# A diffusion backbone on one Trainium2 core: first-layer modulation sums taken from TensorE to ScalarE and GpSimd

## Chip, cores and metric

The kernel runs on one core of a Trainium2 chip. The metric is the device time of one execution in microseconds, lower is better; three executions were timed and their median is used. One more execution was profiled.

## The reference

Two layers of a transformer-like backbone work on 256 latent tokens (`xl`) and 256 context tokens (`xc`) of width 1024. Ahead of each layer a vector of six modulation parts is made for either kind of token, a product of one vector with a 1024 x 6144 matrix:

```python
mod_l = (jax.nn.silu(c) @ ada_w[l] + ada_b[l])[:, None, :]
mod_c = (jax.nn.silu(c_ctx) @ ada_w[l] + ada_b[l])[None, None, :]
sh1_l, sc1_l, g1_l, sh2_l, sc2_l, g2_l = jnp.split(mod_l, 6, axis=-1)
...
hl = modulate(rmsnorm(xl, norm_attn_g[l]), sh1_l, sc1_l)
...
xl = xl + g1_l * yl
xl = xl + g2_l * ffn(modulate(rmsnorm(xl, norm_ffn_g[l]), sh2_l, sc2_l))
```

The change concerns parts 2 to 4 of layer 0: the gate `g1` of the mixer's output, and shift and scale of the second norm. They are wanted only when layer 0's mixer is done; parts 0 and 1 are wanted at once, part 5 and all of layer 1 later.

## The kernel before

Everything is float32. A product is made of three TensorE passes over split operands (`mm3`, L296): weights come as 128 x 1024 tiles (`raw`), ScalarE copies the high part (`whi`, L269) and VectorE subtracts the rest (`wlo`, L270). Layer 0 (`layer0`, L528) projects the 512 normed tokens on 29 column blocks (`proj(m)`, L602): first q and k, then v (L612 to L626, weights `evv`), dt, the scan's input `xBC` (twelve blocks, each followed by a convolution on VectorE, L747 to L753), and z. Between the `xBC` blocks lie the steps of the attention over eight heads (`nattn`, L638): scores on TensorE, bias and maximum on VectorE, exponentials on ScalarE, transposes on TensorE. Behind that come the scan's states (`ssm1`, L817), its output (`ssm2`, L856, where GpSimd makes the tiles `xd` at L895), the output projection and the feed-forward.

The modulation runs in pieces, in the background. `tick()` (L442) takes the next step of the generator `bg`. `ada(0, 1)` (L345) loads sixteen 128 x 1024 tiles of `ada_w` (`araw`, two buffers) and multiplies each on TensorE with the two vectors as stationary operand (`ada_mm`, L313, four matmuls in a tick, each on its own 32 columns of the array); `ada4` (L379) does the same with eight tiles for part 4. `TKP` says after which projections a tick is made, `TKS` that one follows each step of `ssm2`; `need` (L445) draws the rest when a part is wanted. A second generator `bg1` (`ada_sums`, L401) is already written the other way: VectorE multiplies a tile by a column of the vector and adds it to an accumulator (L422, L424), and at the end of a group TensorE only sums over the partitions (L430), followed by four transposes (L371). It serves part 5 of layer 0 and layer 1, and is drawn in the feed-forward.

A scheduler lays down the order of each engine's instructions. All loads go out through one queue (SP), in order; a load that waits for its buffer holds those behind it. The small scratch tiles `hp` have four buffers.

```python
def tick():
    next(bg, None)
...
TKP, TKO, TKS = range(6, 29, 3), 0, 1
```

Of the kernel before, what the change touches and what calls it, by code (L numbers as in the profile page):

```python
# [10 lines left out]
F32 = mybir.dt.float32  # L11
# [7 lines left out]
P = 128  # L19
D = 1024  # L20
KD = 8
# [66 lines left out]
def prepare(x, c, ctx, c_ctx, ada_w, ada_b, norm_attn_g, norm_ffn_g,  # L88
            ev_w_in, ev_w_out, na_rpb, ssm_conv_w, ssm_conv_b, ssm_dt_bias, ssm_a_log, ssm_d, ssm_norm_g,
            ffn_w1, ffn_w3, ffn_w2,  # L90
            od_w_in, od_w_out, swa_sink, ret_log_decay, ret_gn_g, ret_gn_b,
            moe_router, moe_w1, moe_w3, moe_w2, final_g):
    cat = np.concatenate
    A = {}
    A.update(_CT)
    xt = cat([ctx[0], x[0]], axis=0).T
    A["xt"] = xt.reshape(KD, P, 512).transpose(1, 0, 2)
    cc = np.zeros((P, KD, 32), np.float32)
    cc[:, :, 0] = _cols(c_ctx)
    cc[:, :, 1] = _cols(c[0])  # L100
    cc[:, 0, 16] = 1.0
    A["cc"] = cc
    aw = ada_w.reshape(2, KD, P, 3, 2, 2, 512)
    A["ada"] = aw[0].transpose(2, 0, 4, 1, 3, 5).reshape(3, KD, 2, P, 1024)[:2]
    A["ad4"] = aw[0, :, :, 2, 0].reshape(KD, P, 1024)
    ac = aw.reshape(2, 4, 2, P, 3, 2, 2, 512).transpose(0, 4, 6, 5, 1, 3, 2, 7).reshape(2, 3, 4, 4, P, 1024)
    A["adc"] = cat([ac[0, 2, 1::2], ac[1].reshape(12, 4, P, 1024)])
    vec = [_cols(ada_b[0]), _cols(ada_b[1]),
           _cols(norm_attn_g[0]), _cols(norm_attn_g[1]), _cols(norm_ffn_g[0]), _cols(norm_ffn_g[1]),
           _cols(final_g), _cols(ssm_norm_g[0]),  # L110
           _cols(ret_gn_g[0]), _cols(ret_gn_b[0]), _cols(ssm_conv_b[0]),
           ssm_conv_w[0, :, 0, :].reshape(5, 12, P).transpose(2, 1, 0).reshape(P, 60),
           _cols(cat([ssm_dt_bias[0].reshape(-1), np.zeros(96, np.float32)]))]
    ld = ret_log_decay[0]
    vec += [np.repeat(ld.reshape(2, 4, 2).transpose(2, 0, 1), 64, axis=0).reshape(P, 8)]
    A["vec"] = cat(vec, axis=1)
    rows = [ssm_a_log[0].reshape(-1), ssm_d[0], swa_sink[0], ld.reshape(-1)]
    A["row"] = cat(rows)[None, :]
    w = ev_w_in[0]
    q, k, v, z, xbc, dt = np.split(w, np.cumsum([512, 512, 512, 1024, 1536])[:].tolist(), axis=1)  # L120
    dtp = cat([dt, np.zeros((D, 96), np.float32)], axis=1)
    bx = _blocks(cat([q, k, dtp, xbc, z], axis=1))
    bx[:48] = bx[:48].reshape(3, 2, 2, 4, P, P).transpose(2, 0, 1, 3, 4, 5).reshape(48, P, P)
    A["evx"] = _tiles(bx)
    A["evv"] = v.reshape(4, 2, P, 512).transpose(0, 2, 1, 3).reshape(4, P, 1024)
    for i in range(3):
        A["evo%d" % i] = _tiles(_blocks(ev_w_out[0, 512 * i:512 * i + 512]))
    f = cat([ffn_w1[0].reshape(D, NF, 1, P), ffn_w3[0].reshape(D, NF, 1, P)], axis=2).reshape(D, 2 * NF * P)
    A["f13"] = _tiles(_blocks(f))
    A["f2"] = _tiles(_blocks(ffn_w2[0]))  # L130
    w = od_w_in[0]
    q, k, v, rq, rk, rv, rg = np.split(w, np.cumsum([512, 128, 128, 512, 512, 1024])[:].tolist(), axis=1)
    q = q.reshape(D, 2, 4, 64).transpose(0, 2, 1, 3).reshape(D, 512)
    A["odx"] = _tiles(_blocks(cat([k, rk[:, :2 * P], q, v, rk[:, 2 * P:], rq, rg], axis=1)))
    ov = rv.reshape(2, 4, P, 4, 256).transpose(3, 0, 2, 1, 4).reshape(8, P, 1024)
    A["odv"] = ov
    wo = od_w_out[0]
    wq = wo[:512].reshape(2, 4, 64, D).transpose(1, 0, 2, 3).reshape(512, D)
    A["ods"] = _tiles(_blocks(wq))
    A["odr"] = _tiles(_blocks(wo[512:]))  # L140
    q0 = np.arange(256)
    kc = np.arange(64)
    qr, qc = q0 // 64, q0 % 64
    c0 = np.clip(qc - 8, 0, 48)
    ok = (kc[None, :] >= c0[:, None]) & (kc[None, :] < c0[:, None] + 16)
    ci = np.clip(kc[None, :] - qc[:, None] + 15, 0, 30)
    dr = np.arange(4)[None, :] - qr[:, None] + 7
    b = na_rpb[0][:, dr[:, :, None], ci[:, None, :]]
    b = np.where(ok[None, :, None, :], b, np.float32(NEG))
    A["nab"] = b.reshape(8, 2, P, 256).transpose(0, 2, 1, 3).reshape(8, P, 512)  # L150
    A["rt"] = moe_router[0].reshape(KD, P, NE).transpose(1, 0, 2)
    m13 = cat([moe_w1[0].reshape(NE, 1, 2, 4, P, 7, 512), moe_w3[0].reshape(NE, 1, 2, 4, P, 7, 512)], axis=1)
    A["m13"] = m13.transpose(0, 5, 1, 2, 4, 3, 6).reshape(NE, 7, 4, P, 2048)
    m2 = moe_w2[0].reshape(NE, 7, 2, 2, P, 1024)
    A["m2"] = m2.transpose(0, 1, 2, 4, 3, 5).reshape(NE, 7, 2, P, 2048)
    return {k: np.ascontiguousarray(v, dtype=np.float32) for k, v in A.items()}
# [11 lines left out]
def tile_backbone(ctx: ExitStack, tc: tile.TileContext, A, out, upto=99, dbg=None):  # L168
# [2 lines left out]
    NPG, NHP, NW, NA = 22, 4, 3, 2  # L171
    GN0 = 5
    WPRE = (3, 7)
    TKP, TKO, TKS = range(6, 29, 3), 0, 1
    ST = (1, 1, 1, 1, 1, 1, 1, 1, 0, 0)
    ONACT = ((0, 0), (0, 1), (1, 1))
    AHEAD, LEAD, NWT, PRE, SPL = 1, 4, 11, (1, 3, 5, 7), (1, 3)
# [164 lines left out]
            V.scalar_tensor_tensor(gs[:, l, w, s, k0:k1], mod[:, l, s, c0 + k0:c0 + k1], 1.0, vc(gname)[:, k0:k1],  # L342
                                   op0=ALU.add, op1=ALU.mult)

    def ada(l, g):  # L345
        pa = bank("ada")
        for k in range(KD):
            for half in range(2):
                ada_mm(pa, ada_load(l, g, k, half), k, 2 * half)
            yield  # L350
        ada_evac(pa, l, g, (0, 1))
        if g == 0:
            mk_gs(l, 0, "ga%d" % l)
        if g == 2:
            mk_gs(l, 1, "gf%d" % l)

    bgdone = set()

    def background():
        for it, g in ((ada(0, 1), 1), (ada4(), 2)):  # L360
            for _ in it:
                yield
            bgdone.add((0, g))

    def ada_evac2(pa, l, parts):
        n = 32 * len(parts)
# [9 lines left out]
            for s in range(2):  # L376
                V.tensor_tensor(mod[:, l, s, m:m + 4], v[:, s, j], vec[:, o + m:o + m + 4], op=ALU.add)

    def ada4():  # L379
        pa = bank("ada")  # L380
        for k in range(KD):
            raw = araw_tile()
            nc.sync.dma_start(raw, A["ad4"][k])
            ada_mm(pa, raw, k, 2 * (k % 2), 1, 6)
            if k % 2:
                yield
        sb = pool[0].tile([P, 512], F32, tag="nab", name="adas", bufs=2)
        V.tensor_copy(sb, pa)
        pt = bank("ada")
        for b in range(4):  # L390
            for i in range(2):
                T.matmul(pt[:, b * 64:(b + 1) * 64], sb[:, b * P:(b + 1) * P], ident[:, 64 * i:64 * i + 64],
                         start=i == 0, stop=i == 1)
        v = pt[:, 0:256].rearrange("p (b j t) -> p t j b", b=4, t=32)
        o = VOFF["adab0"][0] + 32
        for s in range(2):
            V.tensor_tensor(mod[:, 0, s, 32:40].rearrange("p (j b) -> p j b", j=2), v[:, s],
                            vec[:, o:o + 8].rearrange("p (j b) -> p j b", j=2), op=ALU.add)
        mk_gs(0, 1, "gf0")

    def ada_sums():  # L401
        flat = scc.rearrange("p a b -> p (a b)")
        groups = [(0, (0, 1), [(5, 0), (5, 1)])]
        groups += [(1, (0, 1), [(0, h), (1, h)]) for h in range(2)]
        groups += [(1, (1,), [(g + i, h) for h in range(2) for i in range(2)]) for g in (2, 4)]
        src = iter(range(14))
        for l, who, parts in groups:
            acc = {}
            for j in range(len(parts)):
                n = next(src)  # L410
                for s in who:
                    acc[j, s] = (pm_([P, 512]) if len(acc) < 2 else
                                 pool[0].tile([P, 512], F32, tag="nab", name="acc", bufs=2))
                for kp in range(4):
                    raw = araw_tile()
                    nc.sync.dma_start(raw, A["adc"][n, kp])
                    for k2 in range(2):
                        x = raw[:, k2 * 512:k2 * 512 + 512]
                        for s in who:
                            cs = scc[:, 2 * kp + k2, s:s + 1]  # L420
                            if (kp, k2) == (0, 0):
                                V.tensor_scalar(acc[j, s], x, cs, None, op0=ALU.mult)  # L422
                            else:
                                V.scalar_tensor_tensor(acc[j, s], x, cs, acc[j, s], op0=ALU.mult, op1=ALU.add)  # L424
# [7 lines left out]
            ada_evac2(pa, l, parts)  # L432
            if l and parts[0][0] == 0:
                mk_gs(1, 0, "ga1", 4 * parts[0][1], 4 * parts[0][1] + 4)
            if l and parts[0][0] == 4:
                mk_gs(1, 1, "gf1")
            yield

    bg = background()
    bg1 = ada_sums()  # L440

    def tick():  # L442
        next(bg, None)
# [84 lines left out]
    def layer0():  # L528
# [73 lines left out]
        def proj(m):  # L602
            pp = bank()
            proj_mm(ws, m, 8, hH, hL, pp, 0, 512)
            if m in TKP:
                tick()
            return pp

# [1372 lines left out]
```

## Time and profile before

| | |
|---|---|
| median of three executions | 2102.27 us (2098.06 to 2103.82) |
| the profiled execution | 2096.44 us, span 2094.7 us |
| TensorE (PE) busy over the span | 97% |
| VectorE (DVE), ScalarE (ACT), GpSimd (POOL) | 61%, 43%, 5% |
| mean granted TensorE clock | 0.993 of full speed |

The profiled execution is 5.8 us below the median of the three. A busy share is an average over stages with different limits; the stage that the change touches is the first 350 us.

### The profile page before, as it was taken

The page shows a single profiled execution, that of the slowest core. Times are in us where ns is not written, and L with a number is a line of the kernel's source. Part 1 is how long each engine was busy: PE and PEld are TensorE (multiplying, and loading weights), DVE is VectorE, ACT ScalarE, POOL GpSimd, SP SyncE. Part 2 cuts the span into 40 slices and gives each one's busy share as a digit, 9 for nine tenths or more (in the row PEclk, how much of TensorE's full clock was granted, in tenths as well). Part 3 has the DMA queues.
Part 4 walks back from the last instruction along what each step waited for, and adds up shares of the span by engine and source line. Part 5 has one row for each costly group of instructions (what it writes and reads, how often), then busy time and mean ns, then how long its engine had stood idle before and what let it go on. Part 6 is the DMA issues. An engine that isn't in the chain of part 4 may idle for free. (4 is left out here: it accounts for less than half of the span.)

```text
span 2094.7 us, 26701 instructions
## 1 busy us (share of the span) xinstructions
PE 2026.0 (97%) x10170; PEld 1438.0 (69%) x10170; DVE 1288.0 (61%) x1878; ACT 906.0 (43%) x1296; POOL 109.1 (5%) x148
## 2 busy tenths in 40 slices
PE   7999999889999999999999999999999999999997
PEld 4776756688777878888888888878654554545453
DVE  5366557777566664765477888887644344434443
ACT  4346525643222223544356776767532232232322
POOL 0000015600000000100101000000000000000000
PEclk9999999999999999999999999999999999999998
DMA  8422432025444674322254999999989999999994
GB/s 317 150 94 96 151 121 95 24 68 161 142 150 151 209 236 128 125 61 81 84 228 146 337 364 323 322 334 335 371 352 397 401 406 398 390 418 383 384 361 181
DMA packets 89445, 496.25 MB, mean 237 GB/s; under 512 B 10080, under 2 KB 10848, under 8 KB 46048
## 3 DMA queue, kind: packets, MB, share of 16 engines
q1 hardware_dynamic: 89312, 494.49, 64.3%
q8 instruction: 82, 1.34, 0.3%
q14 instruction: 51, 0.42, 0.1%
HBM read 493.40 MB, written 1.05 MB: 236 GB/s over the span
## 5 line engine op out<-in xcount | busy, mean ns | idle before, releaser
L270 DVE TENSOR_TENSOR w<-w 128x2048 fp32r<-128x2048 f32 (+1 forms) x186 | 384.5, 2081 | 58.7 <-ACT w L269 40.9
L269 ACT ACTIVATE w<-w 128x2048 fp32r<-128x2048 f32 (+1 forms) x186 | 320.5, 1748 | 62.2 <-DVE w L270 35.4
L269 ACT ACTIVATE whi<-raw 128x1024 fp32r<-128x1024 f32 x151 | 160.0, 1060 | 404.1 <-PE bk_mm L298 263.3
L270 DVE TENSOR_TENSOR wlo<-raw,whi 128x1024 fp32r<-128x1024 f32 x151 | 186.6, 1236 | 140.8 <-ACT whi L269 138.3
L297 PE MATMUL bk_mm<-fH,whi 128*128 128x512 f32 (+1 forms) x360 | 140.0, 390 | 2.0 <-DVE xT L518 1.2
L299 PE MATMUL bk_mm<-fH,wlo 128*128 128x512 f32 (+1 forms) x360 | 138.8, 387 | 2.1 <-DVE wlo L270 2.1
L297 PE MATMUL bk_mm<-hH,whi 128*128 128x512 f32 (+1 forms) x384 | 137.5, 361 | 2.2 <-ACT hH L269 2.2
L298 PE MATMUL bk_mm<-fL,whi 128*128 128x512 f32 (+1 forms) x360 | 139.2, 388 | 0.0
L298 PE MATMUL bk_mm<-hL,whi 128*128 128x512 f32 (+1 forms) x384 | 136.2, 355 | 0.0
L299 PE MATMUL bk_mm<-hH,wlo 128*128 128x512 f32 (+1 forms) x384 | 135.5, 354 | 0.0
L1551 PE MATMUL bk_pt<-w,xf 128*64 128x512 f32 x448 | 113.0, 601 | 0.0
L1704 ACT COPY g<-bk_ax 64x512 f32<-64x512 f32 x35 | 20.4, 582 | 207.9 <-PE bk_ax L1551 207.7
L1551 PE MATMUL bk_ax<-w,xf 128*64 128x512 f32 x448 | 107.2, 597 | 0.0
L1763 PE MATMUL bk_mm<-w,gf 128*64 128x512 f32 x448 | 105.3, 597 | 0.0
L1555 PE MATMUL bk_ax<-w,xg 128*128 128x512 f32 x224 | 90.6, 405 | 7.2 <-DVE w L270 7.2
L1554 PE MATMUL bk_ax<-w,xg 128*128 128x512 f32 x224 | 89.6, 400 | 0.0
L1555 PE MATMUL bk_pt<-w,xg 128*128 128x512 f32 x220 | 88.5, 402 | 0.4 <-DVE w L270 0.2
L1556 PE MATMUL bk_ax<-w,xg 128*128 128x512 f32 x224 | 88.8, 396 | 0.0
L456 POOL TENSOR_TENSOR rstd<-rstd,mhalf 128x2 f32<-128x2 f32 (+2 forms) x11 | 10.3, 937 | 1496.1 <-DVE rstd L455 1477.0
L1554 PE MATMUL bk_pt<-w,xg 128*128 128x512 f32 x220 | 88.2, 401 | 0.0
L1556 PE MATMUL bk_pt<-w,xg 128*128 128x512 f32 x220 | 87.5, 398 | 0.0
L297 PEld LDWEIGHTS bk_mm<-hH,whi 128*128 128x128 f32 x384 | 71.8, 188 | 21.8 <-issue 5.4
(568 smaller groups left out, 4357.4 us busy)
## 6 DMA issues: line engine op xcount, KB each, us to landing
w<-in_m SPq DMA_DIRECT2D x334, 1024.0 KB, 7.6
raw<-in_f SPq DMA_DIRECT2D x66, 512.0 KB, 3.7
araw<-in_adc SPq DMA_DIRECT2D x56, 512.0 KB, 3.9
araw<-in_ada SPq DMA_DIRECT2D x32, 512.0 KB, 7.2
raw<-in_evx SPq DMA_DIRECT2D x29, 512.0 KB, 3.7
raw<-in_odx SPq DMA_DIRECT2D x22, 512.0 KB, 3.6
raw<-in_evo SPq DMA_DIRECT2D x12, 512.0 KB, 3.7
xT<-in_xt SPq DMA_DIRECT2D x4, 1024.0 KB, 6.4
```

The costliest lines, as they stand in the source:

```text
L269: a = S.activation(hi, src, AF.Copy)
L270: v = V.tensor_tensor(lo, src, hi.bitcast(F32), op=ALU.subtract)
L297: T.matmul(o, wh, xh, start=first, stop=False)
L298: T.matmul(o, wh, xl, start=False, stop=False)
L299: T.matmul(o, wl, xh, start=False, stop=last)
L456: G.tensor_tensor(r, r, mhalf[:, :n], op=ALU.pow)
L1551: T.matmul(o[c:c + 64], sl(b[0]), wh, start=k < 2, stop=k >= K - 2, tile_position=(0, c))
L1554: T.matmul(o, sl(b[0]), wh, start=first, stop=False)
L1555: T.matmul(o, sl(b[0]), wl, start=False, stop=False)
L1556: T.matmul(o, sl(b[1]), wh, start=False, stop=last)
L1704: S.copy(g[0:64], hb[b][0][64:128])
L1763: T.matmul(accs[0][half][64 * q2:64 * q2 + 64], gT[0][0][:, f, :], wh[:, hs], start=first and q == 0, stop=last and q == 1, tile_position= ...
```

## The change

`ada` as a background step and `ada4` are gone; the tiles of parts 2 to 4 of layer 0 come in the layout of `ada_sums` (`adc`), which gets three groups ahead of the others, of eight tiles each: group 0 is the first half of parts 2 and 3, group 1 their second half, group 2 part 4. There is one generator for all. In the first three groups ScalarE multiplies for the context vector (s = 0) into an `hp` tile, GpSimd multiplies for the latent vector (s = 1) in place and makes both additions, into accumulators that lie in the big pages (`pg`).

```diff
-    TKP, TKO, TKS = range(6, 29, 3), 0, 1
+    TKP, TKO, TKS = {m: 1 if m < 8 else 2 for m in range(6, 19)}, 0, 0
...
-        groups = [(0, (0, 1), [(5, 0), (5, 1)])]
+        groups = [(0, (0, 1), [(2, h), (3, h)]) for h in range(2)]
+        groups += [(0, (0, 1), [(c, 0), (c, 1)]) for c in (4, 5)]
...
+            on = [pg([P, 2, 512], "acc") for _ in range(2)] if n < 3 else None
...
-                            if (kp, k2) == (0, 0):
+                            first = (kp, k2) == (0, 0)
+                            if on:
+                                o = acc[j, s] if first else x if s else hp([P, 512], "adp")
+                                if s:
+                                    G.tensor_scalar(o, x, cs, None, op0=ALU.mult)
+                                else:
+                                    S.activation(o, x, AF.Copy, scale=cs)
+                                if not first:
+                                    G.tensor_tensor(acc[j, s], acc[j, s], o, op=ALU.add)
+                            elif first:
                                 V.tensor_scalar(acc[j, s], x, cs, None, op0=ALU.mult)
...
+            if n in (1, 2):
+                bgdone.add((0, n))
             yield
...
-    bg = background()
-    bg1 = ada_sums()
+    bg = bg1 = ada_sums()
...
-            if m in TKP:
+            for _ in range(TKP.get(m, 0)):
                 tick()
```

Below, the 24 tiles of the three groups are called loads 1 to 24, in program order; a group is two halves of four loads, and a half has its own pair of accumulators.

GpSimd, from the first norm to the second half of group 0. Before, it goes from the norm's `rstd` straight to the scan (`yo`, `xd`):

```order
L456 TENSOR_TENSOR rstd<-rstd,mhalf 128x2 x2
L824 TENSOR_TENSOR yo<-xtok,row 128x1024 x4
L895 TENSOR_SCALAR xd<-xtok,dtp 128x64 x48
```

Now there are 132 instructions of 128 x 512 between the two; these are the last for load 8 and the first for load 9:

```order
L386 TENSOR_SCALAR araw<-araw,scc 128x512
L390 TENSOR_TENSOR acc<-acc,adp 128x512
L390 TENSOR_TENSOR acc<-acc,araw 128x512
L386 TENSOR_SCALAR araw<-araw,scc 128x512
L390 TENSOR_TENSOR acc<-acc,araw 128x512
L386 TENSOR_SCALAR acc<-araw,scc 128x512
```

A load that does not begin a half costs two `TENSOR_SCALAR` and four `TENSOR_TENSOR`, one that begins a half two and two. Each addition reads and writes the accumulator of the one before.

The SP queue in the attention (`nab` is a head's bias, `evx` a weight tile). Before:

```order
L276 DMA raw<-in_evx 128x1024 x3
L307 DMA araw<-in_ada 128x1024
L276 DMA raw<-in_evx 128x1024
L646 DMA nab<-in_nab 128x512
L276 DMA raw<-in_evx 128x1024
L646 DMA nab<-in_nab 128x512 x2
L276 DMA raw<-in_evx 128x1024
L307 DMA araw<-in_ada 128x1024 x2
```

In the changed kernel, from the sixth `nab` on; the loads are 11 to 18:

```order
L617 DMA nab<-in_nab 128x512
L377 DMA araw<-in_adc 128x1024 x2
L617 DMA nab<-in_nab 128x512
L377 DMA araw<-in_adc 128x1024 x2
L275 DMA raw<-in_evx 128x1024
L617 DMA nab<-in_nab 128x512
L377 DMA araw<-in_adc 128x1024
L275 DMA raw<-in_evx 128x1024
L377 DMA araw<-in_adc 128x1024 x3
L275 DMA raw<-in_evx 128x1024
```

Loads 7 and 8 stand behind eight `evx` loads, loads 9 and 10 behind the third `nab`, loads 11 and 12 behind the sixth. With two `araw` buffers a load waits until GpSimd has done with the last but one.

TensorE at the end of group 1 (`bk_ada`, the sums over partitions and their transposes), in the middle of the attention. Before, a tick of four matmuls stands near this place:

```order
L313 MATMUL bk_ada<-araw,scc 32x512 x4
L634 MATMUL bk_ax<-kH,qH 128x512
L635 MATMUL bk_ax<-kL,qH 128x512
L660 MATMUL bk_pt<-ca,Pm 128x128 x4
L636 MATMUL bk_ax<-kH,qL 128x512
```

Now:

```order
L296 MATMUL bk_mm<-hH,whi 128x512
L400 MATMUL bk_ada<-acc,scc 32x512 x2
L631 MATMUL bk_pt<-ca,Pm 128x128 x3
L400 MATMUL bk_ada<-acc,scc 32x512
L631 MATMUL bk_pt<-ca,Pm 128x128
L297 MATMUL bk_mm<-hL,whi 128x512
```

The four sums of a group are the only work that it leaves on TensorE beside four transposes; each waits for GpSimd's last addition to its accumulator, and everything behind it on TensorE waits too. The last sum of group 0 stands behind the first head's scores; that of group 2 stands 78 passes of 128 x 512 and eight transposes behind the last head's output.

## Rows read from the trace of the kernel before

**Rows 1.** Stages: us, then PE, PEld, DVE, ACT, POOL busy (x instructions), granted clock, DMA share, GB/s.

```profile
47.00:250.00 203.00, 202.47 (x979) 144.50 (x978) 117.09 (x197) 108.67 (x185) 0.00 (x0) 1.00 0.41 131
...
300.00:345.00 45.00, 44.47 (x187) 24.28 (x186) 35.38 (x65) 11.83 (x27) 7.47 (x17) 1.00 0.38 121
345.00:402.00 57.00, 51.41 (x372) 36.66 (x370) 46.28 (x87) 45.10 (x119) 54.70 (x86) 0.97 0.09 29
```

**Rows 2.** Waits of PE, 34 to 300 us: waiter <- releaser: us in total, times, longest.

```profile
PE bk_ax L799 <- DVE wx L797: 1.1, 1, 1.1
PE bk_ax L720 <- DVE dtp L715: 0.4, 1, 0.4
```

**Rows 3.** PE timeline, one tick: start us, us, engine, line, out<-in, count.

```profile
72.79 0.39 PE L299 MATMUL bk_mm<-hH,wlo 128*128 128x512 f32 x1
73.11 1.07 PE L313 MATMUL bk_ada<-araw,scc 128*32 128x512 f32 x8
...
74.45 0.40 PE L298 MATMUL bk_mm<-hL,whi 128*128 128x512 f32 x1
```

**Rows 4.** Stage of `ada4`, instructions on `araw` alone: PE, PEld, DVE busy.

```profile
300.00:335.00 35.00, 7.38 (x32) 1.02 (x32) 0.00 (x0) 1.00 0.38 121
```

**Rows 5.** PE timeline, evacuation of `ada4`.

```profile
338.75 1.89 PE L392 MATMUL bk_ada<-ca,adas 128*128 128x64 f32 x16
```

**Rows 6.** PE timeline, passes around a group's sums (first two) and transposes (last two).

```profile
605.51 0.40 PE L299 MATMUL bk_mm<-fH,wlo 128*128 128x512 f32 x1
...
608.00 0.39 PE L298 MATMUL bk_mm<-fL,whi 128*128 128x512 f32 x1
...
608.47 0.39 PE L297 MATMUL bk_mm<-fH,whi 128*128 128x512 f32 x1
...
609.52 0.39 PE L299 MATMUL bk_mm<-fH,wlo 128*128 128x512 f32 x1
```

**Rows 7.** PE timeline: scores by the places of groups 0 and 1, the last head's output.

```profile
133.05 0.28 PE L634 MATMUL bk_ax<-kH,qH 64*128 64x256 f32 x1
...
205.88 0.28 PE L634 MATMUL bk_ax<-kH,qH 64*128 64x256 f32 x1
...
227.69 1.08 PE L686 MATMUL bk_po<-PTc,xT 128*64 128x256 f32 x6
```

**Rows 8.** Groups of POOL by shape: busy us, mean ns, idle before and releasers.

```profile
L912 POOL TENSOR_TENSOR Pm<-Pm 128x512 f32<-128x512 f32 x5 | 6.4, 1275 | 0.8 <-ACT Pm L910 0.8
...
L1518 POOL TENSOR_SCALAR tmp<-xT,rst 128x512 f32<-128x512 f32 x2 | 3.1, 1570 | 0.1
```

**Rows 9.** Groups of ACT by shape, 30 to 250 us: one 128 x 512 copy.

```profile
L269 ACT ACTIVATE hH<-hf 128x512 fp32r<-128x512 f32 x6 | 3.6, 618 | 0.0
```

**Rows 10.** SP timeline: the loads behind which loads 7, 9 and 11 stand.

```profile
118.60 0.33 SPq L276 DMA_DIRECT2D raw<-in_evx  x1
...
132.14 0.33 SPq L646 DMA_DIRECT2D nab<-in_nab  x1
...
166.92 11.01 SPq L646 DMA_DIRECT2D nab<-in_nab  x2
```

**Rows 11.** The page's DMA issues: KB each, median us from issue to landing.

```profile
araw<-in_adc SPq DMA_DIRECT2D x56, 512.0 KB, 3.9
```

**Rows 12.** Line L824, POOL on 128 x 1024: ns min/median/max, starts.

```profile
L824 POOL TENSOR_TENSOR yo<-xtok,row x4: 1898/2126/2877, 263.5 to 270.5; 128x1024 f32<-128x1024 f32 x4
```

**Rows 13.** DVE timeline: one form ahead of those four and during them.

```profile
256.43 0.68 DVE L797 TENSOR_TENSOR wx<-xtok,dtp 128x512 f32<-128x512 f32 x1
...
263.94 2.03 DVE L797 TENSOR_TENSOR wx<-xtok,dtp 128x512 f32<-128x512 f32 x1
```

**Rows 14.** Groups of DVE by shape, 47 to 250 us, that read SBUF alone.

```profile
L270 DVE TENSOR_TENSOR wlo<-raw,whi 128x1024 fp32r<-128x1024 f32 x29 | 35.4, 1222 | 46.0 <-ACT whi L269 46.0
...
L657 DVE TENSOR_SCALAR Pm<-Pm,sm 128x512 f32<-128x512 f32 x16 | 7.7, 479 | 0.1
```

More of the change, by code (lines that the diff above doesn't have):

```diff
@@ L103, in prepare @@
     aw = ada_w.reshape(2, KD, P, 3, 2, 2, 512)
-    A["ada"] = aw[0].transpose(2, 0, 4, 1, 3, 5).reshape(3, KD, 2, P, 1024)[:2]
-    A["ad4"] = aw[0, :, :, 2, 0].reshape(KD, P, 1024)
+    A["ada"] = aw[0].transpose(2, 0, 4, 1, 3, 5).reshape(3, KD, 2, P, 1024)[:1]
     ac = aw.reshape(2, 4, 2, P, 3, 2, 2, 512).transpose(0, 4, 6, 5, 1, 3, 2, 7).reshape(2, 3, 4, 4, P, 1024)
-    A["adc"] = cat([ac[0, 2, 1::2], ac[1].reshape(12, 4, P, 1024)])
+    A["adc"] = cat([ac[0, 1], ac[0, 2, 0::2], ac[0, 2, 1::2], ac[1].reshape(12, 4, P, 1024)])
     vec = [_cols(ada_b[0]), _cols(ada_b[1]),
@@ L343, in mk_gs @@
                                    op0=ALU.add, op1=ALU.mult)
[L345 to L355, printed above, removed]
-    bgdone = set()
[L359 to L363, printed above, removed]
+    bgdone = set()
     def ada_evac2(pa, l, parts):
@@ L377, in ada_evac2 @@
                 V.tensor_tensor(mod[:, l, s, m:m + 4], v[:, s, j], vec[:, o + m:o + m + 4], op=ALU.add)
[L379 to L399, printed above, removed]
     def ada_sums():
         flat = scc.rearrange("p a b -> p (a b)")
-        groups = [(0, (0, 1), [(5, 0), (5, 1)])]
+        groups = [(0, (0, 1), [(2, h), (3, h)]) for h in range(2)]
+        groups += [(0, (0, 1), [(c, 0), (c, 1)]) for c in (4, 5)]
         groups += [(1, (0, 1), [(0, h), (1, h)]) for h in range(2)]
         groups += [(1, (1,), [(g + i, h) for h in range(2) for i in range(2)]) for g in (2, 4)]
-        src = iter(range(14))
-        for l, who, parts in groups:
+        src = iter(range(20))
+        for n, (l, who, parts) in enumerate(groups):
             acc = {}
+            on = [pg([P, 2, 512], "acc") for _ in range(2)] if n < 3 else None
             for j in range(len(parts)):
-                n = next(src)
+                piece = next(src)
                 for s in who:
-                    acc[j, s] = (pm_([P, 512]) if len(acc) < 2 else
+                    acc[j, s] = (on[j][:, s] if on else pm_([P, 512]) if len(acc) < 2 else
                                  pool[0].tile([P, 512], F32, tag="nab", name="acc", bufs=2))
@@ L415, in ada_sums @@
                     raw = araw_tile()
-                    nc.sync.dma_start(raw, A["adc"][n, kp])
+                    nc.sync.dma_start(raw, A["adc"][piece, kp])
                     for k2 in range(2):
@@ L434, in ada_sums @@
                 mk_gs(1, 0, "ga1", 4 * parts[0][1], 4 * parts[0][1] + 4)
-            if l and parts[0][0] == 4:
-                mk_gs(1, 1, "gf1")
+            if parts[0][0] == 4:
+                mk_gs(l, 1, "gf%d" % l)
+            if n in (1, 2):
+                bgdone.add((0, n))
             yield
-    bg = background()
-    bg1 = ada_sums()
+    bg = bg1 = ada_sums()
     def tick():
```

## The prediction

> **What bounds the kernel now.** I read the stages first. From 47 to 250 us, where the projections and the attention lie, TensorE is busy 202.47 of 203 us, while VectorE has 117, ScalarE 109 and GpSimd nothing [rows 1]. The waits say the same: from 34 to 300 us TensorE waits for anyone only 1.5 us in all [rows 2]. So here a microsecond of TensorE is a microsecond of the kernel, in both directions: what leaves TensorE is gained, and what TensorE must wait for is lost. Behind that, from 300 to 345 us, TensorE is still full (44.47 of 45), and from 345 to 402 us GpSimd is (54.7 of 57, the tiles `xd`), with TensorE at 51 [rows 1]. The granted clock is 1.00 in the stretch that the change touches, the upper of the two levels, 2.4 GHz.
>
> **What TensorE gives up.** One tick lies between two passes that start at 72.79 and 74.45; without it they would be two pitches of 0.23 apart, so a tick costs 1.66 - 0.47 = 1.2 us [rows 3]. The eight ticks of `ada(0, 1)` are 9.6 us. The tile's rows in the stage of `ada4` sum to 7.4 us [rows 4]. The evacuations are 1.8 us for `ada4` (1.89 less a little overlap, [rows 5]) and by the same rate about 0.4 us for the four transposes of `ada(0, 1)`. Together 19.2 us go.
>
> **What TensorE takes on.** A group's sums lie between passes at 605.51 and 608.00, which is 2.49 - 0.47 = 2.0 us, and its transposes between 608.47 and 609.52, 0.6 us [rows 6]. Three groups are 7.8 us. The net is 19.2 - 7.8 = **11.4 us** less work on TensorE. The least that this can be worth is 2.2 us, if GpSimd's stage from 345 us starts no earlier for it (the 9.2 us of `ada4` and its evacuation lie right ahead of that stage). I take 11.4, because TensorE is full up to that stage and the output projection is there to fill it.
>
> **What hides nothing or little.** VectorE gets three small evacuations for two. ScalarE gets 48 copies at 0.62 us [rows 9], 30 us beside the 109 that it works in 203 us: room enough, unless a copy stands in its queue and waits for its load. The bytes loaded are the same.
>
> **GpSimd is the price.** The trace has both of its operations at just this size: an addition takes 1.275 us, a multiplication by a column 1.57 us [rows 8]. A load costs two of these and four of those, 8.2 us; one that begins a half 5.7 us. A half of four loads is 30.4 us, the three groups 182 us. That looks as if it fitted into the 203 us, but the loads come late and the sums stand early:
>
> - *Group 0.* Loads 7 and 8 stand behind the weight load issued at 118.60 [rows 10], some 3 us earlier without the ticks, and land 3.9 us later [rows 11], at 120. They take 16.5 us, until 136.5. TensorE is at the last sum at about 132 (the place is just behind the scores that start at 133.05 [rows 7], less some 4 us of ticks, plus the sums made by then). It waits 4 us.
> - *Group 1.* Loads 11 and 12 stand behind the sixth `nab`, 166.92 before [rows 10]; with the ticks gone, group 0's sums and its wait this is 170, landed at 174. GpSimd has by then finished loads 9 and 10 and stood idle. From here it never stops, as a load lands within 3.9 us of a buffer becoming free and 8.2 us of work lie in the other. Loads 11 to 16 take 46.9 us, until 221. TensorE reaches the last sum, close behind the scores at 205.88 [rows 7], at 207, with the first wait 211. It waits 10 us more.
> - *Group 2.* Eight loads are 60.8 us, until 282. Its last sum lies 78 passes of 0.23 us and eight transposes behind the last head's output at 227.69 [rows 7], which makes 248, and 262 with the 14 us waited. It waits 20 us more.
>
> That is 34 us of waiting against 11.4 gained: **+22 us** at the bare prices. Behind the waiting sum nothing on TensorE can pass; the attention, the weight loads behind an `araw` load on SP, and the scan's `yo` on GpSimd all come later with it and add little of their own, since TensorE is the one that waits.
>
> **VectorE beside GpSimd.** Bare prices hold only if the two do not hinder each other. They do in places: four GpSimd instructions that take 1.90 us at best took 2.26 on the mean and 2.88 at worst [rows 12], and a VectorE product of two SBUF tiles took 2.03 instead of 0.68 us in their midst [rows 13]. The additions of 1.275 us showed no such thing [rows 8]. The Trainium skill (SBUF — State Buffer, the section "SBUF: two separate sides") says that GpSimd shares a port pair with VectorE, held by one of them for a whole instruction, while the other is blocked fully. The 2.03 us agrees with it; by it alone every VectorE instruction of that kind would stop GpSimd for its length.
>
> The bounds come from rows. The two largest kinds of VectorE work that read SBUF alone are 35.4 + 7.7 = 43.1 us in 203 [rows 14], 21%. If none of it hinders GpSimd, the prices are bare; if all of it does, they are 1 / 0.79 = 1.27 times as long. I take half, 1.12, between the untouched additions and the 1.19 of 2.26 over 1.90. With 1.12 the same walk ends group 0 at 138.5 (6.5 us waited), group 1 at 229 against 213.5 (15.5), group 2 at 297 against 270 (27): 49 - 11.4 = +38 us. Between +22 and +38 I forecast **+30 us**. Made against the profiled execution this is 2096.4 + 30 = 2126; the median of the three is 5.8 us higher, so I say **2132 us**, with 2124 to 2149 as the forecast's own range (its upper end is +38 with the 9.2 us not regained).
>
> **Rivals.**
>
> *GpSimd keeps up; faster.* If the 44 instructions of group 2 fit between TensorE's two places, 207 and 248, that is 0.93 us each, no sum waits and the 11.4 us are gained: 2091 us. For it speaks that the order has them there, that GpSimd is empty in this stretch, and that its rows are rough. Against it speaks that both prices are measured at this very size, at 1.275 and 1.57. It decides at a mean of 0.93 us where I count 1.38.
>
> *The waits just eat the gain; no change.* At 1.1 us each, group 2 takes 48 us, the sums wait some 11 us in all, and the time is about 2102 us. The same rows speak against it.
>
> *Full hindrance; slower still.* With 1.27 group 0 ends at 141 (9 us waited), group 1 at 239 against 216 (23), group 2 at 316 against 280 (36): 68 - 11.4 = +56, 2158 us. For it: GpSimd is always busy here, so that each `wlo` and each softmax product meets it, and ScalarE's copies for a late load stand ahead of the next head's exponentials. Against it: the additions of [rows 8] lay beside a VectorE busy 46 of 57 us [rows 1] and were not lengthened, and a TensorE that waits gives VectorE less to do.
>
> **Chances and range.** Forecast 0.53, full hindrance 0.20, no change 0.10, GpSimd keeps up 0.17. A measurement of this kernel tells some 0.3%, 6.3 us, from no change; so faster 0.17, within 0.10, slower 0.73. The range is 2097 to 2168: it leaves out the case that GpSimd keeps up (0.17), reaches down to no change, and up to 2158 and 10 us more for what the coupled queues may add.
>
> **What the profile would show.** If I am right: GpSimd near 10 tenths from about 170 to 280 us, with some 1.3 us an addition and 1.6 a multiplication; TensorE's largest waits on the sums L400, released by GpSimd's L390, least in group 0 and most in group 2; the stage from the last head's output on some 30 us later, and the feed-forward unchanged in length. If the multiplications and additions are below 1 us, or TensorE waits less than 11 us on L400, the forecast is wrong. If TensorE waits instead for exponentials or weights, with ScalarE behind a copy of L388, the size may be right and the step wrong.

## The result and the profile after

| | before | after |
|---|---|---|
| median of four executions | 2103.05 us (2098.06 to 2104.6) | 2170.48 us (2168.42 to 2175.4) |
| profiled execution, span | 2096.44, 2094.7 us | 2168.9, 2167.1 us |
| ratio | | 1.0337, 95% interval 1.0323 to 1.0351 |
| GpSimd busy over the span | 5% | 14% |

The change makes the kernel 67.4 us slower. I forecast slower, at 2132 us with a range up to 2168: the sign was right, the size was less than half.

The place of the loss comes from the starts of the same instructions in both traces, asked line by line:

| instruction | before | after | later by |
|---|---|---|---|
| first scores | 127.3 | 131.5 | 4.2 |
| start of the last product of the last head's output | 228.4 | 269.2 | 40.8 |
| first `wx` product on TensorE | 267.3 | 338.5 | 71.2 |
| first `xd` on GpSimd | 328.3 | 394.0 | 65.7 |
| last `xd` | 400.2 | 466.5 | 66.3 |
| span's end | 2094.7 | 2167.1 | 72.4 |

So the loss is made up to the first `xd`, and is kept. (The last 6 us lie in later stages that run the same instructions in both; the medians, 67.4 apart, hardly have them.)

These are the windows between those places after the change, in the columns of [rows 1]; before, TensorE was busy 202.47 of 203 us here:

```profile
30.00:131.50 101.50, 95.05 (x440) 73.34 (x438) 42.79 (x59) 46.51 (x66) 48.76 (x32) 0.97 0.49 166
131.50:269.20 137.70, 113.70 (x512) 74.92 (x512) 81.53 (x147) 78.18 (x148) 96.85 (x67) 0.86 0.27 88
269.20:338.50 69.30, 47.36 (x188) 32.35 (x187) 22.79 (x45) 25.29 (x50) 51.20 (x37) 0.78 0.38 129
338.50:394.00 55.50, 54.31 (x196) 36.13 (x195) 38.91 (x55) 11.97 (x16) 6.71 (x4) 1.00 0.18 57
```

TensorE stood idle 6.5 + 24.0 + 21.9 + 1.2 = 53.6 us, against 2.2 us before up to the same place (328.3 us). Its granted clock is also down, to 0.97, 0.86 and 0.78 in the first three of these windows. If each window of half a microsecond from 30 to 394 us is taken by itself, and its busy time is multiplied by one less the granted clock, the sum says that 21.5 us of TensorE's work time were lost to the lower clock, and none before. The work itself fell by 7.2 us (busy less that loss: 288.9 against 296.1). That is 51.4 + 21.5 - 7.2 = 65.7 us, as in the table.

What TensorE waited for, 34 to 420 us (the columns of [rows 2]):

```profile
PE bk_ada L400 <- POOL acc L390: 38.1, 7, 15.5
PE bk_mm L593 <- ACT xT L597: 5.6, 1, 5.6
PE bk_ax L605 <- ACT Pm L626: 5.0, 2, 2.8
```

And the waits themselves on TensorE's timeline, one or two per group (start, us, and in brackets the idle time before it):

```profile
146.17 1.92 PE L400 MATMUL bk_ada<-acc,scc 128*32 128x512 f32 x4 [8.02 <-POOL acc L390]
...
242.23 1.92 PE L400 MATMUL bk_ada<-acc,scc 128*32 128x512 f32 x4 [7.40 <-POOL acc L390]
...
282.91 1.91 PE L400 MATMUL bk_ada<-acc,scc 128*32 128x512 f32 x2 [4.26 <-POOL acc L390]
...
314.10 1.92 PE L400 MATMUL bk_ada<-acc,scc 128*32 128x512 f32 x4 [15.45 <-POOL acc L390]
```

The clock around the first of them, in windows of 4 us:

```profile
134.00:138.00 4.00, 4.00 (x20) 2.88 (x18) 3.95 (x9) 3.04 (x7) 4.00 (x4) 1.00 0.57 169
138.00:142.00 4.00, 0.15 (x1) 0.00 (x0) 0.90 (x2) 0.00 (x0) 4.00 (x3) 0.91 0.07 27
142.00:146.00 4.00, 0.00 (x0) 0.00 (x0) 0.00 (x0) 0.00 (x0) 4.00 (x4) 0.50 0.41 114
...
150.00:154.00 4.00, 3.72 (x9) 1.87 (x10) 1.34 (x3) 0.58 (x1) 1.76 (x2) 0.50 0.38 131
154.00:158.00 4.00, 4.00 (x19) 2.22 (x17) 1.83 (x7) 2.17 (x6) 0.00 (x0) 0.89 0.00 0
```

TensorE idles from 138 us on, the clock goes to 0.50 (1.2 GHz), and stays there while TensorE works again, until about 155 us.

GpSimd's groups by shape, 0 to 420 us, in the columns of [rows 8]:

```profile
L386 POOL TENSOR_SCALAR araw<-araw,scc 128x512 f32<-128x512 f32 x42 | 70.1, 1670 | 65.1 <-ACT adp L388 65.1
L390 POOL TENSOR_TENSOR acc<-acc,araw 128x512 f32<-128x512 f32 x42 | 60.0, 1430 | 1.4
L390 POOL TENSOR_TENSOR acc<-acc,adp 128x512 f32<-128x512 f32 x42 | 57.6, 1371 | 42.2 <-ACT adp L388 40.3 <-ACT acc L388 1.6
...
L386 POOL TENSOR_SCALAR acc<-araw,scc 128x512 f32<-128x512 f32 x6 | 9.5, 1584 | 0.0
```

Together 197.2 us, 1.08 times the 182 of the bare prices. The surprise is on the right: GpSimd, which should be the bound, was itself idle 105 us until ScalarE's products came. Of these, 33.0 us lie ahead of its first instruction at 48.31 us, and 69.8 us in three long waits, which end where these rows start (GpSimd's timeline); the last row is its last addition:

```profile
117.13 4.77 POOL L386 TENSOR_SCALAR araw<-araw,scc 128x512 f32<-128x512 f32 x3 [31.17 <-ACT adp L388]
...
181.71 1.28 POOL L390 TENSOR_TENSOR acc<-acc,adp 128x512 f32<-128x512 f32 x1 [29.95 <-ACT adp L388]
...
256.48 1.29 POOL L390 TENSOR_TENSOR acc<-acc,adp 128x512 f32<-128x512 f32 x1 [8.66 <-ACT adp L388]
...
316.89 1.26 POOL L390 TENSOR_TENSOR acc<-acc,araw 128x512 f32<-128x512 f32 x1
```

The first of these waits is 31 us long though its load had been issued at 85.99 us. SP's timeline, and then ScalarE's:

```profile
85.99 0.33 SPq L377 DMA_DIRECT2D araw<-in_adc  x1
86.41 8.91 SPq L275 DMA_DIRECT2D raw<-in_evv  x4
```

```profile
92.65 1.06 ACT L268 ACTIVATE whi<-raw 128x1024 fp32r<-128x1024 f32 x1 [9.10 <-DMA raw<-in_evv]
...
114.79 1.06 ACT L268 ACTIVATE whi<-raw 128x1024 fp32r<-128x1024 f32 x1 [4.08 <-PE bk_mm L297]
115.75 0.67 ACT L667 ACTIVATE dtT<-bk_mm,vec 128x512 f32<-128x512 f32 x1
116.32 1.32 ACT L388 ACTIVATE adp<-araw,scc 128x512 f32<-128x512 f32 x2
...
153.28 0.58 ACT L632 COPY xT<-bk_pt 128x512 f32<-128x512 f32 x1 [15.41 <-PE bk_pt L631]
```

ScalarE's order has the product behind the `whi` copies of v and dt, which wait for TensorE. And the weights of v (`evv`) stand on SP behind the `araw` load, which waited until 85.99 for GpSimd's buffer: ScalarE waits 9.1 us for them and TensorE 5.6 (L593 above). Ahead of GpSimd's second long wait ScalarE itself stood 15.4 us, until 153.28, for transposes that lie on TensorE behind the waiting sums of group 0; the product that GpSimd waits for then starts at 180.9 us. So each engine waits for the others in turn.

### The profile page after: what moved, and what is told of

The parts are those of the page before. It is cut to its first block, busy times and chain, and to the rows that moved or that the text cites. A ratio compares the mean times of both kernels' runs of the same rounds, so it can differ in the third digit from the quotient of the medians.

```text
span 2167.1 us, 26779 instructions
## 1 busy us (share of the span) xinstructions
PE 2039.2 (94%) x10090; PEld 1451.5 (67%) x10090; DVE 1298.4 (60%) x1885; ACT 932.8 (43%) x1342; POOL 303.6 (14%) x280
## 5 line engine op out<-in xcount | busy, mean ns | idle before, releaser
L297 PE MATMUL bk_mm<-hL,whi 128*128 128x512 f32 (+1 forms) x384 | 141.4, 369 | 0.0
L1526 PE MATMUL bk_pt<-w,xg 128*128 128x512 f32 x220 | 88.6, 403 | 0.4 <-DVE w L269 0.2
L1525 PE MATMUL bk_pt<-w,xg 128*128 128x512 f32 x220 | 88.4, 402 | 0.5 <-DVE xg L1511 0.5
L297 PEld LDWEIGHTS bk_mm<-hL,whi 128*128 128x128 f32 x384 | 75.2, 196 | 18.9 <-issue 8.4
```

The lines of the kernel that those rows point to most:

```text
L297: T.matmul(o, wh, xl, start=False, stop=False)
L1525: T.matmul(o, sl(b[0]), wh, start=first, stop=False)
L1526: T.matmul(o, sl(b[0]), wl, start=False, stop=False)
```

## The experiments

Times are medians, compared with the kernel before on the same chip; the changed kernel itself is 1.0337.

| experiment | us | ratio (95%) |
|---|---|---|
| e1_fill | 2194.27 | 1.0435 (1.0417 to 1.0452) |
| e2_late | 2153.94 | 1.0244 (1.0222 to 1.0266) |
| e3_act | 2143.25 | 1.0192 (1.0175 to 1.0209) |
| e4_vec | 2119.56 | 1.0081 (1.0065 to 1.0098) |
| e5_pages | 2184.17 | 1.0401 (1.0381 to 1.0422) |
| e6_late_vec | 2108.66 | 1.0037 (1.0022 to 1.0052) |
| e7_pages_late | 2144.80 | 1.0201 (1.0176 to 1.0226) |
| e8_from8 | 2174.33 | 1.0354 (1.0333 to 1.0374) |
| e9_defer | 2159.04 | 1.0270 (1.0245 to 1.0296) |
| e10_defer_split | 2131.25 | 1.0140 (1.0110 to 1.0169) |
| e11_defer_vec | 2118.47 | 1.0078 (1.0053 to 1.0103) |
| e12_nopool | 2098.29 | 0.9992 (0.9978 to 1.0006) |
| e13_doors | 2177.64 | 1.0370 (1.0352 to 1.0387) |
| e14_part4 | 2105.92 | 1.0031 (1.0018 to 1.0043) |
| e15_half | 2113.45 | 1.0056 (1.0036 to 1.0075) |
| e16_fill0 | 2181.52 | 1.0389 (1.0363 to 1.0415) |

The forecast of the theory came true in e12 alone. The times of e1, e2, e7, e9, e10, e13 and e14 lie where the rival had them (in e10 without its sign, additions above 1.5 us: they took 1.40), those of the other eight in neither range.

The scheduler lays down the order of all engines anew for each kernel, so a run differs from the changed kernel in more than its edit. Counted in the traces in projection passes (`bk_mm`), the last sum of group 2 on TensorE stands behind 544 of them in the changed kernel, 504 in e12, 532 in e16 and 720 in e9. A difference of some 10 us between two of these kernels can't be put down to one edit.

**How much GpSimd does: e12, e15, e3.**

```diff
 e12_nopool: no GpSimd work
-if s: G.tensor_scalar(o, x, cs, None, op0=ALU.mult)
-else: S.activation(o, x, AF.Copy, scale=cs)
-if not first: G.tensor_tensor(acc[j, s], acc[j, s], o, op=ALU.add)
+if first or not s: S.activation(o, x, AF.Copy, scale=cs)
 e3_act: GpSimd adds only
-if s: G.tensor_scalar(o, x, cs, None, op0=ALU.mult)
-else: S.activation(o, x, AF.Copy, scale=cs)
+S.activation(o, x, AF.Copy, scale=cs)
 e15_half: as e3_act, and
-if not first: G.tensor_tensor(...)
+if s and not first: G.tensor_tensor(...)
```

> The changed kernel without GpSimd's part: its 48 multiplications and 84 additions are left out (the first product of each accumulator is made by ScalarE, the others are lost, so the sums are not the reference's). Loads, ScalarE's copies, ticks and TensorE's sums stay. Theory (everything lost is GpSimd's pace, through whatever queue it reaches TensorE): the gain of TensorE's lighter work is all that is left, 2090 to 2102. Rival (the copies on ScalarE and the loads in SP's queue at these places cost by themselves): 2115 or more.

> The changed kernel with both multiplications on ScalarE (48 more copies of 0.71 us, 34 us) and only the 84 additions on GpSimd: a load costs GpSimd 5.5 us instead of 8.2. Theory (GpSimd's time for a load sets the waits): the waits on the sums shrink from 38 us to about 10 and the low clock with them: 2115 to 2135. Rival (ScalarE and the queues behind it): ScalarE has twice the copies ahead of its other work, so 2170 to 2190.

> The arrangement of e3_act (all products on ScalarE) with only the additions of the latent vector left on GpSimd: 42 of 84, some 57 us; the context vector's other products are lost, so the sums are not the reference's. Between e12_nopool (no GpSimd work, 2098) and e3_act (84 additions, 115 us, 2143). If the cost follows GpSimd's work from the first microsecond: halfway, 2118 to 2124. If there is a point up to which GpSimd keeps pace with the loads and costs nothing: 2097 to 2106.

Without GpSimd the time is that of the kernel before, 0.9992. Loads, ScalarE's products (six more of them) and TensorE's sums are made as in the changed kernel, the sums at earlier places, and TensorE's waits from 30 to 330 us are 3.8 us; 227.5 to 270 us (the second row) is the only stretch with a lower clock before `xd`:

```profile
125.80:227.50 101.70, 101.70 (x515) 70.27 (x514) 72.23 (x144) 75.18 (x146) 0.00 (x0) 1.00 0.38 122
227.50:270.00 42.50, 40.15 (x181) 29.41 (x180) 22.51 (x46) 25.92 (x51) 2.66 (x2) 0.96 0.54 179
```

So nearly all of the 67.4 us comes with GpSimd's part, its work and the waits on it, and the 54 products and the loads cost nothing that can be told by themselves. With 57.8 us of GpSimd work (42 additions) the ratio is 1.0056, with 118.0 us (84 additions) 1.0192, with 197.2 us 1.0337: over the kernel before, some 12, 40 and 71 us by these ratios. So neither line of e15 holds: it lies between free and halfway. But these are not steps of GpSimd's work alone: e15 and e3 make all 96 products on ScalarE, at 0.71 us each, and no run has the 96 without GpSimd. In e15 TensorE waits 5.7 us at the sums and 5.0 us for ScalarE's `BT` (30 to 340 us). e3 missed the forecast (2115 to 2135): its waits at the sums did fall to 14.9 us, but 9.4 us of waiting for the scan's `BT` came in their place.

**Sums that stand too early: e9, e2.** e9 postpones only the sums and what follows them; e2 spreads the ticks.

```diff
 e9_defer: in ada_sums, groups 0 to 2
-pa = bank("ada"); ...sums...; ada_evac2(pa, l, parts)
+owed.append(sums)
 and need() ends with
+while owed: owed.pop(0)()
 e2_late
-TKP = {m: 1 if m < 8 else 2 for m in range(6, 19)}
+TKP = {m: 2 if m == 6 else 1 for m in range(6, 29)}
```

> The changed kernel with the sums over partitions of the three groups written later: groups 0 and 1 where the output projection wants the gate, group 2 where the second norm wants its shift and scale. Loads, copies, products and additions stay as in the changed kernel. Theory (TensorE stands at sums that come too early in its order, 38 us, and its clock falls for it): those waits and the low clock after them go, the 15 us of other waits stay: 2110 to 2120. Rival (GpSimd's pace reaches TensorE also through ScalarE, whose copies wait in one queue with the exponentials): 2140 or more.

> The changed kernel with the same 24 steps, but one after each of projections 6 to 28 (two after 6) instead of two after each of 8 to 18: same work on ScalarE, GpSimd and SP, later sums. Theory (GpSimd's 197 us do not fit between the loads and the early sums): GpSimd now has 300 us, TensorE waits less than 5 us on the sums, the clock stays up: 2090 to 2100, under the kernel before by the work that left TensorE. Rival (ScalarE's copies ahead of the exponentials and the loads that hold the weight loads behind them are what costs): these are all still there, so no better than 2150.

My theory fell here. In e9 no wait of TensorE at a sum is left, and yet only 11 us come back (14 by the ratios). Up to the first `xd`, now at 379.2 us, TensorE is still idle 46.9 us and loses 20.1 us to the low clock, summed as above. It now waits for ScalarE, 30 to 340 us:

```profile
PE bk_pt L760 <- ACT BT L757: 14.3, 2, 8.5
PE bk_po L665 <- ACT xT L640: 6.7, 2, 4.1
PE bk_mm L601 <- ACT xT L605: 5.1, 1, 5.1
```

and ScalarE, in front of that very `BT`, for a load:

```profile
273.85 1.33 ACT L389 ACTIVATE adp<-araw,scc 128x512 f32<-128x512 f32 x2 [4.98 <-DMA araw<-in_adc]
275.09 0.71 ACT L757 ACTIVATE BT<-cacc,vec 128x512 f32<-128x512 f32 x1
```

and that load, on SP, for a buffer that GpSimd has not given back (30 to 340 us):

```profile
SPq L378 <- POOL acc L391: 152.4, 21, 11.2
```

The same wait goes round by another way. e2 brings 17 us: 19.1 us of waits at the sums are left, the wait for the weights of v stays (5.8 us), and part of GpSimd's work now lies beside `xd` (first `xd` 387.5 us).

**More buffers: e5, e7, e13; a later start: e8.**

```diff
 e5_pages (e7_pages_late: with e2's TKP too)
-raw = araw_tile()
+raw = pg([P, 1024], "araw") if on else araw_tile()
 e13_doors: e5_pages, e9_defer and
-hp([P, 512], "adp")
+pg([P, 512], "adp")
 e8_from8
-TKP = {m: 1 if m < 8 else 2 for m in range(6, 19)}
+TKP = {m: 2 for m in range(8, 20)}
```

> The changed kernel with the 24 tiles of the three groups in the big pages instead of the two araw buffers: a load no longer waits on SP for GpSimd to give a buffer back, and holds no weight load behind it. All work and the ticks as in the changed kernel. Theory now (the two buffers on the one SP queue tie the engines together: GpSimd stands idle 70 us for loads between 48 and 318 us and then TensorE for GpSimd): GpSimd's idle time there falls under 30 us, the wait for the weights of v goes, and half of the 66 us with it: 2120 to 2140. Rival (GpSimd's pace alone, 8 us a load, against sums that stand too early): the waits on the sums stay, 2155 to 2170.

> The changed kernel with both the big pages for the tiles and one tick after each projection; ScalarE and GpSimd do the same work. Theory (buffers and early sums are the whole cost): TensorE waits under 10 us on the sums and the time is 2090 to 2110. Rival (GpSimd and ScalarE in the stream of a full TensorE cost in any arrangement, by ScalarE's copies that stand ahead of other copies): 2125 or more.

> GpSimd does all its work, but the three ways by which others wait for it are opened together: tiles and ScalarE's products in the big pages (as e5_pages, and the products too), sums written late (as e9_defer). Theory (GpSimd's pace alone, reaching TensorE by sums, by the two tile buffers on SP or by ScalarE's queue, so that closing one way moves the wait to another): with all three open TensorE hardly waits, 2095 to 2115. Rival (one engine's work among the others costs in any arrangement): 2130 or more.

> The changed kernel with its ticks begun two projections later: two after each of projections 8 to 19, none after 6 and 7. Theory (loads 5 and 6 hold the weights of v behind them on SP while GpSimd works, 5.6 us of TensorE's idle time and some 3 us of low clock): that wait goes, but loads and sums of group 0 come later, and GpSimd has as much to do up to sums that stand two projections later: 2155 to 2170. Rival (the start does not matter): 2168 to 2173.

None helped where I expected it. e5 is slower than the changed kernel: GpSimd starts at 62.5 us instead of 48.3, when a load issued on SP at 57.6 us has landed, and it still idles 28.6 us (for a load) and 27.0 us (for ScalarE) in the two places of before. Nor did the pages free SP's queue, which waits for GpSimd 84.3 us from 30 to 345 us, against 155.7 us in the changed kernel:

```profile
SPq L377 <- POOL acc L390: 84.3, 9, 18.9
```

e7 is some 9 us better than e2. e8 (2174, above both forecasts) loses the wait for v, but TensorE still waits 37.6 us at the sums. In e13 all three ways were to be open, but SP still waits 95.2 us for GpSimd, and 6.0 us are left at a sum. TensorE's waits from 30 to 345 us, and then the longest of them followed back on the timelines of TensorE, VectorE and ScalarE:

```profile
PE bk_mm L296 <- DVE cacc L730: 23.5, 2, 21.7
```

```profile
287.41 0.77 PE L296 MATMUL bk_mm<-hH,whi 128*128 128x512 f32 x1 [21.66 <-DVE cacc L730]
```

```profile
282.58 5.34 DVE L730 SCALAR_TENSOR_TENSOR cacc<-bk_mm,vec,cacc 128x508 f32<-128x508 f32 x8 [8.75 <-ACT cacc L727]
```

```profile
270.30 0.72 ACT L389 ACTIVATE acc<-araw,scc 128x512 f32<-128x512 f32 x1 [6.28 <-DMA araw<-in_adc]
...
278.71 0.72 ACT L389 ACTIVATE adp<-araw,scc 128x512 f32<-128x512 f32 x1 [6.14 <-DMA araw<-in_adc]
...
281.86 1.26 ACT L727 ACTIVATE cacc<-bk_mm,vec 128x512 f32<-128x512 f32 x2 [0.50 <-POOL acc L391]
```

TensorE waits for a bank that VectorE's convolution still has to read, VectorE for ScalarE's `cacc`, and ScalarE stands in front of it at products whose loads are late: the way through SP and ScalarE again. A new one follows behind: `Btok` takes a page that GpSimd still reads from, and VectorE waits 19.9 us for it, until 307.8 us. Closing ways one by one did not end it; taking the work away (e12) does.

**The clock: e1, e16.** Filler, passes that are overwritten, is laid ahead of the sums so that TensorE does not rest while GpSimd finishes.

```diff
 before the sums of a group (e16: of group 0 alone, 52 passes)
+T.matmul(pa[0:32, :], scc[:, 0, :], lastc, start=True, stop=True)
+for _ in range((36, 36, 72)[n]):
+    T.matmul(pa, filler[0](0, 0, P), filler[0](0, 0, 512), start=True, stop=True)
```

> The changed kernel with filler ahead of each of the three groups' sums on TensorE: one small product that reads ScalarE's last copy of the group, then 36, 36 and 72 passes of 128 x 512 (8, 8 and 17 us at 0.23 us a pass) into the bank that the sums overwrite. Theory (the waits for GpSimd cost twice, once as idle time and once because the granted clock is 0.50 in them and for some microseconds after): the filler takes no time that was not idle, the clock stays at 1.00 there, and most of the 21.6 us that passes at the lower level cost come back: 2150 to 2156. Rival (only the length of the waits counts, the clock is a side show): TensorE stands at the same sums until GpSimd is done, so 2168 to 2173, or slower by the filler that lies ahead of other work.

> The changed kernel with filler in group 0 alone, 52 passes (12 us) where e1_fill had 36, so that no rest of the wait is left. Theory (the low clock comes on top of the wait): the filler takes only idle time, and the passes behind it run at 1.00 instead of 0.50, so 1 to 5 us less than the changed kernel: 2165 to 2170. Rival (the filler delays the loads and copies behind it as much as it gains): 2170 to 2178.

In e16 the filler does locally what the theory says. The windows of the wait:

```profile
138.00:142.00 4.00, 4.00 (x18) 3.00 (x17) 3.03 (x6) 0.78 (x2) 4.00 (x4) 1.00 0.31 89
...
150.00:154.00 4.00, 4.00 (x20) 1.42 (x18) 0.68 (x1) 0.34 (x1) 3.40 (x3) 1.00 0.23 55
154.00:158.00 4.00, 4.00 (x23) 3.17 (x22) 1.92 (x7) 1.76 (x6) 0.00 (x0) 1.00 0.21 80
```

The clock is 1.00 where it was 0.50, and the transposes of group 0 start at 153.99 us instead of 154.88. Yet the kernel is 11 us slower than the changed one. Up to its first `xd` (409.1 us) TensorE is idle 53.4 us and loses 22.6 us to the low clock, summed as above, against 53.6 and 21.5 us in the changed kernel: what was filled and kept up in group 0 came back at later places, and the work is 14.2 us more, 12.1 us of it the filler. In e1 the filler was 3 us too short for group 0; the clock fell to about 0.57 behind that rest. So the low clock is real on TensorE, but in neither run did the filler make the kernel faster; that GpSimd's chain sets the pace there is my reading, not tested. I had put the two down as added costs; these runs show neither that they add nor that they don't.

**VectorE in GpSimd's place: e4, e6, e10, e11, e14.**

```diff
 e4_vec (e6: with e2's TKP; e11: and with e9's late sums)
 V.scalar_tensor_tensor(acc[j, s], x, cs, acc[j, s], op0=ALU.mult, op1=ALU.add)  for both s
 e10_defer_split: the same for s = 0 alone, GpSimd keeps s = 1; late sums
 e14_part4: parts 2 and 3 by ada(0, 1) on TensorE, part 4 as one group on VectorE
+TKP = {m: 1 for m in (*range(6, 21, 2), *range(21, 29))}
```

> The changed kernel with the products of the three groups on VectorE, in one instruction each (multiply and add, 0.75 us on 128 x 512), as the later groups do it: 96 of them, 72 us, and none on ScalarE or GpSimd; ticks as in the changed kernel. Theory (GpSimd's pace): a load takes 3.0 us of VectorE instead of 8.2 of GpSimd; VectorE is 117 us busy of 203 there and has the room; the sums wait less than 10 us in all: 2090 to 2110. Rival (the load order on SP and the early sums are to blame whoever multiplies): the first of the 38 us stay, 2140 to 2170.

> The products on VectorE as in e4_vec, and the ticks one after each projection as in e2_late. Theory (with 300 us instead of 200 VectorE has room for 72 us more, and a load gives its buffer back after 3 us): TensorE keeps its gain, 2090 to 2102. Rival (VectorE is too full wherever it is put: wlo and the softmax wait behind the products): 2110 to 2120 as in e4_vec.

> As e9_defer, and ScalarE left out: VectorE makes the products and sums of the context vector (48 instructions of 0.75 us or less), GpSimd those of the latent vector alone (5.7 us a load, 137 us in all). Theory (early sums, and copies and loads in ScalarE's queue, are all that cost): TensorE keeps its gain, 2092 to 2102. Rival (GpSimd and VectorE hinder each other on SBUF): GpSimd's additions above 1.5 us on the mean and 2110 or more.

> As e6_late_vec (all products on VectorE, one tick after each projection), with the sums written later as in e9_defer. Theory: TensorE's remaining waits in e6_late_vec were for VectorE's other work and not for sums, so little changes: 2103 to 2109. Rival (the sums' places cost there too): 2091 to 2100.

> Another arrangement: parts 2 and 3 stay on TensorE as in the kernel before (eight ticks after projections 6 to 20, every second), part 4 alone goes to VectorE as one group (24 us of products beside projections 21 to 28, and TensorE's 9.2 us become 2.6). Theory (VectorE has room there and nobody waits): 2094 to 2100. Rival (what leaves TensorE ahead of GpSimd's xd is not regained, or VectorE's products are in the way): 2100 to 2110.

All are far better than the changed kernel and none beats the one before. e6, the best with all three groups moved, has its first `xd` at 329.5 us against 328.3: what TensorE saves goes into small waits (6.5 us in three for VectorE's `wx`, 2.1 us in two for exponentials) and order. The late sums of e11 make that worse. In e14 the first `xd` is at 328.5 us, unchanged, and the last at 406.4 instead of 400.2. In e10 GpSimd's work for one of the two vectors (153 us) and VectorE's for the other cost 1.4%, where VectorE's work for both costs 0.8% in e4 and in e11; e10 and e4 have the ticks of the changed kernel, e11 those of e2.

## Why the prediction was wrong

Against the +30 us of the forecast stand, up to the first `xd`: 38.1 us of waits at the sums (34 to 49 in the walk), 13.3 us more of added idle time (taken as little), 21.5 us of low clock (taken as nothing), less 7.2 us of work (taken as 11.4).

**Right: where it would be lost, and GpSimd's price.** GpSimd took 1.08 times the bare prices; I took 1.12. TensorE's largest waits were on the sums, released by GpSimd, 9.1 us in group 0, 8.8 in group 1, 20.3 in group 2 (forecast 6.5, 15.5, 27 at 1.12), so most in group 2, though not least in group 0. The feed-forward is unchanged in length. Against 49 us of waiting at 1.12 stand 51.4 us of added idle time. That agreement is partly luck, since a quarter of it lay elsewhere.

**Wrong: the attention, the weight loads and the scan "add little of their own, since TensorE is the one that waits".** This step let waits run one way, from GpSimd to TensorE. The traces show them going round: GpSimd holds a tile, SP holds the next load and the weights behind it, ScalarE holds `BT` and the exponentials behind a product whose load is late, TensorE waits, and with it the next `whi` copies and the next products for GpSimd. e9 is the test: the waits at the sums gone, 11 of 67 us regained, 46.9 us idle elsewhere. The last lines of the prediction named this case (the size right, the step wrong, ScalarE behind a copy of L388); its sum has no price for it, its range 10 us.

**Wrong: GpSimd's start.** I let its work begin when a load lands. It began when ScalarE's product came up in ScalarE's order: 31.2 and 30.0 us of idle time in two places. It ended at 318 us, not 297.

**Left out: the clock.** I read a granted clock of 1.00 in this stretch and left it at that, though the waits that I added were of a kind that the trace of before had none of here. TensorE lost 21.5 us of work to the lower level, the largest single term that the sum did not have. In e16, where the clock was kept up in group 0, as much was lost at later places (22.6 us), so how much of it would come back with the waits as they are stays open.

**Oversized: the gain.** I took 11.4 us. TensorE's work fell by 7.2 us up to `xd`, and e12, where hardly anything waits, is 2.2 us faster, which can't be told from no change (0.9992, interval 0.9978 to 1.0006). I had given 2.2 us as the lower bound for an `xd` stage that starts no earlier; it started earlier by 2.8 us only (325.5 us). By e12 the rival in which GpSimd keeps up would have been about 2098, no change, and not 2091 (an estimate, since e12's sums stand at other places).

**VectorE beside GpSimd.** I took 1.12 for it, and 1.08 came. VectorE was hindered too. From 47 to 345 us:

```profile
L628 DVE TENSOR_SCALAR Pm<-Pm,sm 128x512 f32<-128x512 f32 x16 | 13.2, 822 | 0.2
```

This took 479 ns before [rows 14] and 822 now; in e12, without GpSimd's work, it took 481. Over the same stretch `wlo`, which reads two SBUF tiles, took 1271 ns on the mean against 1230, and the convolution, which reads PSUM, about 740 in both. The Trainium skill (SBUF — State Buffer, "SBUF: two separate sides") says that a VectorE instruction with two SBUF inputs and a GpSimd instruction that reads SBUF can't hold the port pair that they share at the same time, and that the second to start waits for all of the first. The means of this trace hardly show that for `wlo`; whether GpSimd's 1.08 is the other side of it was not tested. Neither is a large part of the loss.

## What to carry to other kernels

Before work moves to an idle engine, ask for each of its instructions which in-order queue its inputs come through and which buffer it holds until it is done, and follow the wait once all the way round; an engine with 66% of a stretch in work (197 of 300 us) can't be counted on to hide its work if its inputs come out of a queue that waits for the full engine. Leaving the moved work out altogether (e12) costs one run and tells about how much the change can be worth (here 2 us, by its interval at most some 5), and whether the loss comes with the moved work at all. A wait that disappears from the list without the time following it has only moved: look at who is waited for next.

## What the runs showed that I had not expected

- 57.8 us of additions spread over some 300 us, on an engine that otherwise stood empty, together with 42 more products on ScalarE than e12 has, cost 0.56%, about 12 us.
- A wait of TensorE of 8 us was followed by some 9 us at 0.50 of the clock, in which TensorE worked again (146 to 155 us). In e1 a wait of 3.1 us was followed by windows of 4 us at 0.58 and 0.56.
- More room made it no faster: with the tiles in pages instead of two buffers the ratio was 1.0401 against 1.0337, and SP still waited 84.3 us for GpSimd.

What stays open: ScalarE's products were not moved ahead of the `whi` copies by themselves, nor the loads' order on SP, so the 61 us in which GpSimd stood idle for them are read from the trace and were not tested; how much of the 67 us each of the ways round and the low clock carry alone can't be told, as they stand in for one another; and no run held the scheduler's order fixed while GpSimd's work was changed.
